# Operands of a 256-token float32 chain moved to chosen places within 256 bytes, with one raw weight buffer fewer and new sequences of matmul passes

## The chip, the cores and the metric

The kernel runs on one core of a Trainium2 chip. The metric is the device time of one execution in microseconds. Three runs of the kernel before gave 797.72, 798.06 and 798.28, median 798.06.

## The reference

Two blocks follow one another on 256 tokens of width 1024, all in float32. Cut to what matters:

```
# first block
q,k,va, qr,kr,vr, gr, ga,gb = split(rms(x) @ w_in)
y  = sigmoid(ga)*(diff_attention(q,k,va) @ wd) + sigmoid(gb)*(silu(gr)*retention(qr,kr,vr) @ wr)
x += y @ wo
x += relu(rms(x) @ w_ff1)**2 @ w_ff2                # 1024 -> 4096 -> 1024: f1, f2
x += sigmoid(rms(x) @ w_pg) * (p @ wp)
x  = rms(x)
# second block
x += (mlstm(rms(x) @ [mq, mk, mv, mo, gates])) @ mw
u, v = causal_conv3(rms(x) @ [ug, uv])              # 2 x 2816 columns
x += (silu(u) * v) @ dn                             # 2816 -> 1024
out = rms(x)
```

## The kernel before

The weights are cut into slabs, mostly of 1024 rows by 256 columns, and each slab into two halves of 128 partitions by 1024 floats (512 KB), 257 halves and 140 MB in all. The order of the halves (`order`) is fixed by a plan. Every half goes through four hands:

- SP's queue carries it from HBM to a tile `raw` (L155, 5 buffers);
- ACT copies it, rounded, to a tile `hi` of type float32r (L167, 6 buffers);
- DVE subtracts: `lo` = raw - hi, float32r too (L179, 6 buffers);
- PE multiplies. The activations are split into a high and a low tile in the same way (hh and hl, h2h and h2l, and so on), and a product is three passes of 256 columns for each 128 rows: high weights with high activations, high weights with low activations, low weights with high activations. So a whole slab of 1024 x 256 takes 48 matmuls of 256 columns, a half slab 24.

In `pe_b` (L230 to L232) the slab's tiles are the stationary operand (weights) and the activations the moving one; q, k, qr, kr, ga, gb, wd, wr, wo, f1, f2, pg, mq, mk, mw, ug, uv go through it. In `pe_a` (L242 to L244) it is the other way round: activations stationary, the slab moving; va, vr, gr, mv, mo. In the down projection dn (`pe_down`, L1366 to L1368) the slab moves as well, in pieces of 512 and 256 columns, over gh and gl. In the profile an operand pair reads `out<-moving,stationary`. The weights of a matmul are loaded by an instruction of their own (PEld in the profile) while the matmul ahead of it runs.

`slot()` is called after each half slab: it lets ACT run to 6 halves ahead of the last half used up (`high_to`), moves the work that waits behind a slab on by a step, and lets DVE do the same (`split_to`). Each subtraction sets free one raw tile, upon which SP issues the transfer of the half five places on (`dma_to(state["split"] + NRAW)`). `at(name, ...)` hangs other work on a slab: its first function puts matmuls on PE after the slab (with `mid=True` after the first half), its second the work of ACT and DVE behind them. `gates2` makes the tile me for the gates of the mLSTM, `gates3_pe` transposes gi and me (L1082, tile pa_g), `gates3_post` copies pa_g to acol (L1087), `decay_pe` and `decay_post` (L1100, L1109) read it for the decay matrix dm.

The tile framework puts the buffers of a pool behind one another. In the built program raw, hi and lo tiles of 4,096 bytes per partition all begin at 128 modulo 256. The "big" tiles, which hold the activations, are 8,224 bytes long, so that each begins 32 bytes further modulo 256 than the one ahead. The place of the operands, in bytes modulo 256, before and after:

| slabs | role of the activations | activations before (high, low) | slab before | activations after | slab after (hi, lo) |
|---|---|---|---|---|---|
| wo | moving | mh 96, ml 160 | 128 | 0 | 192, 64 |
| f1 | moving | h2h 160, h2l 192 | 128 | 0 | all 16 pairs of 0, 64, 128, 192, one per slab |
| f2, third block of rows | moving | ah 128, al 192 | 128 | 0 | all 16 pairs, one per slab |
| mw | moving | hsh 192, hsl 64 | 128 | 0 | 192, 64 |
| ug, uv 2 to 10 | moving | h7h 0, h7l 192 | 128 | 0 | the 16 pairs, two of them twice |
| q, k, qr, kr, ga, gb, pg and the rest of `pe_b` | moving | various multiples of 32 | 128 | 0 | 192, 64 |
| va, vr, gr | stationary | hh 192, hl 160 | 128 | 0 | spread over the pairs |
| mo, mv 1 to 3 | stationary | h4h 32, h4l 224 | 128 | 0 | spread over the pairs |
| dn, second eight blocks of rows | stationary | gh 64, gl 192 | 128 | 0 | spread over the pairs |

Of the kernel before, what the change touches and what calls it, by code (L numbers as in the profile page):

```python
# [10 lines left out]
F32 = mybir.dt.float32  # L11
F32R = mybir.dt.float32r
# [4 lines left out]
P = 128  # L17
T = 256
# [2 lines left out]
LAM_INIT = 0.8 - 0.6 * math.exp(-0.3 * 0)  # L21
LNEXP = "natural_log_exp_and_others"
NBUF = 6
NRAW = 5
NWARM = 9
NRAWUP = 2
JOINT = (("q0", "k0"), ("wo0", "wo1"), ("f1_0", "f1_1"), ("pg0", "pg1"), ("mq0", "mk0"), ("mw0", "mw1"), ("ug0", "uv0"))
NUP = 2816 // 256
NPAR = 65 + 176 + 2

GAINS = [
    ("g_mix", 8), ("g_mlp", 8), ("g_ple", 8), ("g_final", 8), ("l0_norm_mix_2", 8), ("l0_norm_ffn_2", 8),
# [62 lines left out]
def _rows(slab):  # L95

    name, w, k0, nk, cl = slab
    return ((0, 1), (2, 3, 4), (5, 6, 7)) if name == "mv0" else (tuple(range(nk // 2)), tuple(range(nk // 2, nk)))


def _width(slab):
    return 264 if slab[0] == "mv0" else 2048 // slab[3]


@with_exitstack
def block_kernel(ctx: ExitStack, tc: tile.TileContext, I, out):
# [7 lines left out]
    psum = ctx.enter_context(tc.tile_pool(name="psum", bufs=4, space=bass.MemoryType.PSUM))  # L114

    def bigt(name, dt=F32, cols=2048):
        return big.tile([P, 2056], dt, tag="big", name=name)[:, 0:cols]

    def c8(t):
        return t.rearrange("p (c t) -> p c t", t=T)  # L120
# [1 line left out]
    def mmbank(name):  # L122
        return psum.tile([P, 512], F32, tag="mm", name=name)
# [21 lines left out]
    def geometry(i):  # L145
        return len(_rows(slabs[i])[0]), _width(slabs[i])

    def dma_to(n):
        while state["dma"] < min(n, len(order)):
            i, s = order[state["dma"]]  # L150
            name = slabs[i][0]
            kk, cw = len(_rows(slabs[i])[s]), _width(slabs[i])
            raw = wpool.tile([P, 1024], F32, tag="raw", name=f"raw_{name}_{s}", bufs=NRAW)
            v = raw[:, 0:kk * cw].rearrange("p (k n) -> p k n", k=kk)
            nc.sync.dma_start(out=raw[:, 0:kk * cw], in_=I["w"][state["dma"], :, 0:kk * cw])  # L155
            raw_t[i, s] = v
            state["dma"] += 1

    def high_to(n):

        while state["high"] < min(n, len(order)):
            i, s = order[state["high"]]
            kk, cw = len(_rows(slabs[i])[s]), _width(slabs[i])
            dma_to(state["high"] + 1)
            hi = wpool.tile([P, 1024], F32R, tag="hi", name=f"hi_{slabs[i][0]}_{s}", bufs=NBUF)
            hi_t[i, s] = hi[:, 0:kk * cw].rearrange("p (k n) -> p k n", k=kk)
            S.activation(hi_t[i, s], raw_t[i, s], ACTF.Copy)  # L167
            state["high"] += 1

    def split_to(n):  # L170

        while state["split"] < min(n, len(order)):
            i, s = order[state["split"]]
            kk, cw = len(_rows(slabs[i])[s]), _width(slabs[i])
            high_to(state["split"] + 1)
            raw = raw_t.pop((i, s))
            lo = wpool.tile([P, 1024], F32R, tag="lo", name=f"lo_{slabs[i][0]}_{s}", bufs=NBUF)
            lo_t[i, s] = lo[:, 0:kk * cw].rearrange("p (k n) -> p k n", k=kk)
            V.tensor_tensor(out=lo_t[i, s], in0=raw, in1=hi_t[i, s].bitcast(F32), op=ALU.subtract)  # L179
# [40 lines left out]
    def pe_b(ps, i, xh, xl, ks, m, start, stop):  # L220

        kk, cw = geometry(i)
        mc = min(P, cw)
        o = ps[0:mc, m * T:(m + 1) * T]
        for k in ks:
            hv, lv = hi_t[i, k // kk], lo_t[i, k // kk]
            a, x = k % kk, k
            sl = slice(m * P, m * P + mc)
            st, sp = start and k == ks[0], stop and k == ks[-1]
            TE.matmul(o, lhsT=hv[:, a, sl], rhs=xh[:, x, :], start=st, stop=False, skip_group_check=True)  # L230
            TE.matmul(o, lhsT=hv[:, a, sl], rhs=xl[:, x, :], start=False, stop=False, skip_group_check=True)  # L231
            TE.matmul(o, lhsT=lv[:, a, sl], rhs=xh[:, x, :], start=False, stop=sp, skip_group_check=True)  # L232

    def pe_a(ps, i, xh, xl, ks, t, start, stop):

        o = ps[:, t * T:(t + 1) * T]
        ts = slice(t * P, (t + 1) * P)
        for k in ks:
            hv, lv = hi_t[i, k // 4], lo_t[i, k // 4]
            a = k % 4  # L240
            st, sp = start and k == ks[0], stop and k == ks[-1]
            TE.matmul(o, lhsT=xh[:, k, ts], rhs=hv[:, a, :], start=st, stop=False, skip_group_check=True)  # L242
            TE.matmul(o, lhsT=xl[:, k, ts], rhs=hv[:, a, :], start=False, stop=False, skip_group_check=True)
            TE.matmul(o, lhsT=xh[:, k, ts], rhs=lv[:, a, :], start=False, stop=sp, skip_group_check=True)  # L244
# [3 lines left out]
    def at(name, pe=None, post=None, off=0, mid=False):  # L248
        i = index[name] + off
        if mid:  # L250
            hooks_mid.setdefault(i, []).append((pe, post))
            return
        if pe:
            hooks_pe.setdefault(i, []).append(pe)
        if post:
            hooks_post.setdefault(i, []).append(post)
# [23 lines left out]
                        later(i, g)  # L280
                slot()

    def step_b(name, xh, xl, post):
        i = index[name]
        ps = mmbank(f"ps_{name}")

        def piece(s):
            for m in range(2):
                pe_b(ps, i, xh, xl, range(4 * s, 4 * s + 4), m, s == 0 and m == 0, s == 1 and m == 1)

        halves(i, piece)
        after(i, lambda: post(ps))
# [73 lines left out]
    with tc.manual_schedule():  # L366
# [1 line left out]

        x = bigt("x0")
        xT = c8(x)  # L370
        par = const.tile([P, NPAR], F32, name="par")
        nc.scalar.dma_start(out=par[:, 0:8], in_=I["par"][:, 0:8])
        first = [wpool.tile([P, 1024], F32, tag="raw", name=f"raw_{n}", bufs=NRAW) for n in range(4)]
        for c in range(4):
# [83 lines left out]

        sq_new("n1")
        for n in range(4):  # L460
            for tag, dt, d in (("hi", F32R, hi_t), ("lo", F32R, lo_t)):
                t = wpool.tile([P, 1024], dt, tag=tag, name=f"{tag}_{n}", bufs=NBUF)
                d[order[n]] = t.rearrange("p (k n) -> p k n", k=4)
        def first_split(n, ks):
            rv, hv, lv = first[n].rearrange("p (k n) -> p k n", k=4)[:, ks, :], hi_t[order[n]][:, ks, :], lo_t[order[n]][:, ks, :]
            S.activation(hv, rv, ACTF.Copy)
# [111 lines left out]
        va = bigt("va").rearrange("p (t n) -> p t n", t=2)  # L578
# [146 lines left out]
        i, ps0 = index["q0"], [mmbank(f"ps_{n}") for n in ("q0", "k0")]  # L725
# [44 lines left out]
        gr, ga = bigt("gr").rearrange("p (t n) -> p t n", t=2), c8(bigt("ga"))  # L770
# [119 lines left out]
        ah, al = {}, {}  # L890
# [27 lines left out]
        for j in range(4):  # L918
            ps = mmbank(f"ps_f2_{j}")
            for kg in range(4):  # L920
                i = index[f"f2_{j}_{kg}"]

                def piece(s):
                    for m in range(2):
                        pe_b(ps, i, ah[kg], al[kg], range(4 * s, 4 * s + 4), m, kg == 0 and s == 0 and m == 0,
                             kg == 3 and s == 1 and m == 1)

                halves(i, piece)
                after(i, *([lambda j=j, ps=ps: post_res("n3", j, h3h, h3l, "g_ple", r2)(ps)] if kg == 3 else []))
# [5 lines left out]
        i = index["wp"]  # L935
        need(i, 0)
        need(i, 1)
        for j in range(4):
            ps = mmbank(f"ps_wp{j}")
            for m in range(2):  # L940
                o = ps[:, m * T:(m + 1) * T]
                sl = slice((2 * j + m) * P, (2 * j + m + 1) * P)
                for k in range(2):
                    hv, lv = hi_t[i, k], lo_t[i, k]
# [335 lines left out]
        ug, uv = {}, {}  # L1280
# [22 lines left out]
        def post_ug(j):  # L1303
            def f(ps):
                yield from conv(ps, 2 * j, 2 * j, f"g{j}")
                y = ug[j] = pr(ring[:, (2 * j) % 4, :])
                S.activation(y, y, ACTF.Silu)
                if j == NUP - 1:
                    S.preload_act_table_set(LNEXP)
            return f  # L1310

        def post_uv(j):
            def f(ps):
                yield from conv(ps, 22 + 2 * j, 2 * j + 1, f"v{j}")
# [213 lines left out]
```

## Time and profile before

| | |
|---|---|
| median of three runs | 798.06 us |
| the profiled execution | 797.67 us |
| its span | 795.9 us |
| matmuls, and PE's busy time | 6,394, 785.8 us |
| weight loads, busy time | 6,394, 771.2 us |
| DVE, ACT busy | 569.5 us, 464.6 us |
| carried by SP's queue and the others | 141.75 MB, mean 178 GB/s |

The span is what the profile's views cover; the other 1.8 us of the execution lie around it. A matmul's duration in the timeline covers its way through the array and overlaps the next one's, so the cost of a matmul in a long row is the distance from start to start.

### The profile page before, as it was taken

Reading aid. Unit: us, or ns where it says so; the run is one execution under the profiler, and the core shown is the slowest. Engines: PE = TensorE matmul, PEld = TensorE weight load, DVE = VectorE, ACT = ScalarE, POOL = GpSimd, SP = SyncE. Lnnn points to the kernel's source line nnn. Section 1 sums busy time; section 2 is a strip of 40 time slices with the busy share of each in tenths; the row PEclk is TensorE's granted clock in tenths of the full one; section 3 lists DMA queues with packets and bytes.
Section 4 is the critical chain, followed back from the end, with each engine's and each line's share of the span. In section 5 each row is a group of like instructions: output and inputs, shape, how many; then the busy total and the mean of one; then the engine's idle time right before and its main releaser. Section 6 shows DMA issues by size and latency. Waiting matters only on the chain.

```text
span 795.9 us, 15702 instructions
## 1 busy us (share of the span) xinstructions
PE 785.8 (99%) x6394; PEld 771.2 (97%) x6394; DVE 569.5 (72%) x895; ACT 464.6 (58%) x788; POOL 2.2 (0%) x8
## 2 busy tenths in 40 slices
PE   8999999999999999999999999999999999999996
PEld 8999999999999999999999999999999999999885
DVE  6877889566666577666555557897978988987443
ACT  7655656765744456555444456765865766756432
POOL 0000000000000000000000000000000000000000
PEclk9999999999999999999999999999999999999998
DMA  8875453455666556666665545354365457765621
GB/s 305 269 242 161 152 160 123 150 162 163 186 199 189 167 184 192 192 185 188 202 183 184 187 145 179 129 202 157 120 223 160 144 177 234 220 206 163 208 80 53
DMA packets 40472, 141.75 MB, mean 178 GB/s; under 512 B 4640, under 2 KB 5024, under 8 KB 40400
## 3 DMA queue, kind: packets, MB, share of 16 engines
q1 hardware_dynamic: 40032, 140.02, 55.7%
q8 instruction: 50, 0.82, 0.4%
q0 software_dynamic: 224, 0.72, 0.2%
q14 instruction: 22, 0.18, 0.1%
q10 hardware_dynamic: 144, 0.00, 0.0%
HBM read 139.68 MB, written 1.05 MB: 177 GB/s over the span
## 4 chain that ended last, share of the span: by engine, by line
PE 94%; DVE 3%; ACT 1%; DMA 1%; issue 1%; SPq 0%; DVEq 0%
PE ps_f L231 8%; PE ps_f L230 8%; PE ps_f L232 8%; PE ps_uv L230 3%; PE ps_ug L230 3%; PE ps_uv L231 3%; PE ps_ug L231 3%; PE acc L1368 3%; PE acc L1366 3%; PE acc L1367 3%; PE ps_ug L232 3%; PE ps_uv L232 3%; PE ps_vr L242 1%; PE ps_wo L231 1%; PE ps_va L242 1%; PE ps_mo L242 1%
## 5 line engine op out<-in xcount | busy, mean ns | idle before, releaser
L179 DVE TENSOR_TENSOR lo_f<-raw_f,hi_f 128x1024 fp32r<-128x1024 f32 x64 | 77.7, 1223 | 52.8 <-ACT hi_f L167 52.8
L167 ACT ACTIVATE hi_f<-raw_f 128x1024 fp32r<-128x1024 f32 x64 | 67.6, 1060 | 79.6 <-PE ps_f L231 70.3
L231 PE MATMUL ps_f<-al,hi_f 128*128 128x256 f32 x256 | 72.1, 282 | 0.0
L230 PE MATMUL ps_f<-ah,hi_f 128*128 128x256 f32 x256 | 72.0, 281 | 0.0
L232 PE MATMUL ps_f<-ah,lo_f 128*128 128x256 f32 x256 | 72.0, 281 | 0.0
L230 PE MATMUL ps_f<-h2h,hi_f 128*128 128x256 f32 x256 | 71.9, 281 | 0.0
L231 PE MATMUL ps_f<-h2l,hi_f 128*128 128x256 f32 x256 | 71.9, 281 | 0.0
L232 PE MATMUL ps_f<-h2h,lo_f 128*128 128x256 f32 x256 | 71.8, 281 | 0.0
L230 PEld LDWEIGHTS ps_f<-ah,hi_f 128*128 128x128 f32 x256 | 48.3, 189 | 0.0
L230 PEld LDWEIGHTS ps_f<-h2h,hi_f 128*128 128x128 f32 x256 | 48.3, 189 | 0.0
L232 PEld LDWEIGHTS ps_f<-ah,lo_f 128*128 128x128 f32 x256 | 48.3, 189 | 0.0
L231 PEld LDWEIGHTS ps_f<-al,hi_f 128*128 128x128 f32 x256 | 48.2, 188 | 0.0
L231 PEld LDWEIGHTS ps_f<-h2l,hi_f 128*128 128x128 f32 x256 | 48.1, 188 | 0.0
L232 PEld LDWEIGHTS ps_f<-h2h,lo_f 128*128 128x128 f32 x256 | 48.1, 188 | 0.0
L179 DVE TENSOR_TENSOR lo_dn<-raw_dn,hi_dn 128x1024 fp32r<-128x1024 f32 x22 | 26.9, 1223 | 22.8 <-ACT hi_dn L167 22.8
L167 ACT ACTIVATE hi_dn<-raw_dn 128x1024 fp32r<-128x1024 f32 x22 | 23.3, 1060 | 30.7 <-PE acc L1367 24.5
L230 PE MATMUL ps_ug<-h7h,hi_ug 128*128 128x256 f32 x144 | 40.8, 283 | 0.0
L230 PE MATMUL ps_uv<-h7h,hi_uv 128*128 128x256 f32 x144 | 40.5, 282 | 0.0
L231 PE MATMUL ps_uv<-h7l,hi_uv 128*128 128x256 f32 x144 | 40.3, 280 | 0.0
L231 PE MATMUL ps_ug<-h7l,hi_ug 128*128 128x256 f32 x144 | 40.3, 280 | 0.0
L232 PE MATMUL ps_ug<-h7h,lo_ug 128*128 128x256 f32 x144 | 40.0, 278 | 0.0
L232 PE MATMUL ps_uv<-h7h,lo_uv 128*128 128x256 f32 x144 | 40.0, 278 | 0.0
(492 smaller groups left out, 2932.4 us busy)
## 6 DMA issues: line engine op xcount, KB each, us to landing
raw_f<-in_w_dram SPq DMA_DIRECT2D x64, 512.0 KB, 3.6
raw_ug<-in_w_dram SPq DMA_DIRECT2D x22, 512.0 KB, 4.1
raw_uv<-in_w_dram SPq DMA_DIRECT2D x22, 512.0 KB, 4.3
raw_dn<-in_w_dram SPq DMA_DIRECT2D x22, 512.0 KB, 3.6
raw_va<-in_w_dram SPq DMA_DIRECT2D x8, 512.0 KB, 4.8
raw_vr<-in_w_dram SPq DMA_DIRECT2D x8, 512.0 KB, 3.5
raw_gr<-in_w_dram SPq DMA_DIRECT2D x8, 512.0 KB, 3.5
raw_ga<-in_w_dram SPq DMA_DIRECT2D x8, 512.0 KB, 3.6
```

The source lines that it names most:

```text
L167: S.activation(hi_t[i, s], raw_t[i, s], ACTF.Copy)
L179: V.tensor_tensor(out=lo_t[i, s], in0=raw, in1=hi_t[i, s].bitcast(F32), op=ALU.subtract)
L230: TE.matmul(o, lhsT=hv[:, a, sl], rhs=xh[:, x, :], start=st, stop=False, skip_group_check=True)
L231: TE.matmul(o, lhsT=hv[:, a, sl], rhs=xl[:, x, :], start=False, stop=False, skip_group_check=True)
L232: TE.matmul(o, lhsT=lv[:, a, sl], rhs=xh[:, x, :], start=False, stop=sp, skip_group_check=True)
L242: TE.matmul(o, lhsT=xh[:, k, ts], rhs=hv[:, a, :], start=st, stop=False, skip_group_check=True)
L1366: TE.matmul(o, lhsT=gh[b][:, r, ts], rhs=hv[:, 0, ns], start=k == 0, stop=False)
L1367: TE.matmul(o, lhsT=gl[b][:, r, ts], rhs=hv[:, 0, ns], start=False, stop=False)
L1368: TE.matmul(o, lhsT=gh[b][:, r, ts], rhs=lv[:, 0, ns], start=False, stop=k == NK - 1)
```

## The change

1. All buffers get known places. The big tiles grow from 2,056 to 2,112 columns, and the tile par by 32, so that every big, raw, hi and lo buffer begins at 0 modulo 256.
2. The slots for hi and lo grow from 1,024 to 1,088 columns, and a slab's hi and lo tiles begin 0, 64, 128 or 192 bytes into their slots, by a function of the slab's name (`_place`, in units of 64 bytes): hi at 192 and lo at 64 where nothing else is said, and through all sixteen pairs in f1, f2, ug and uv from 2 on, the five kinds of `pe_a`, and dn.
3. The raw buffers go from five to four.
4. f2, and ug and uv from 2 on, run their passes in two other sequences (`pe_b2`). With f1, which keeps its triples, there are three.
5. The transposes of the gates go from the end of mv1 to the middle of mv2, 24 matmuls later.

The number of matmuls, weight loads, copies, subtractions and transfers stays.

PE at the start of f2, on its first 128 rows, before (ps_f2_0 is the bank of the first 256 output columns, ah0 and al0 the high and low activations, hi_f2_0_0_0 and lo_f2_0_0_0 the first half slab):

```order
L230 MATMUL ps_f2_0_4760<-ah0_3822,hi_f2_0_0_0_4603 128x256
L231 MATMUL ps_f2_0_4760<-al0_3823,hi_f2_0_0_0_4603 128x256
L232 MATMUL ps_f2_0_4760<-ah0_3822,lo_f2_0_0_0_4607 128x256
L230 MATMUL ps_f2_0_4760<-ah0_3822,hi_f2_0_0_0_4603 128x256
L231 MATMUL ps_f2_0_4760<-al0_3823,hi_f2_0_0_0_4603 128x256
L232 MATMUL ps_f2_0_4760<-ah0_3822,lo_f2_0_0_0_4607 128x256
```

and after (x2 is two matmuls in a row, one for each 128 of the 256 columns):

```order
L268 MATMUL ps_f2_0_4758<-ah0_3820,hi_f2_0_0_0_4601 128x256 x2
L268 MATMUL ps_f2_0_4758<-ah0_3820,lo_f2_0_0_0_4605 128x256 x2
L268 MATMUL ps_f2_0_4758<-al0_3821,hi_f2_0_0_0_4601 128x256 x2
L268 MATMUL ps_f2_0_4758<-ah0_3820,hi_f2_0_0_0_4601 128x256 x2
L268 MATMUL ps_f2_0_4758<-ah0_3820,lo_f2_0_0_0_4605 128x256 x2
```

The moving tile changes after four matmuls and again after two, where it changed twice in three; high and low weights take turns in pairs.

PE at the start of ug2 (bank ps_ug2, activations h7h and h7l), before:

```order
L230 MATMUL ps_ug2_7839<-h7h_7529,hi_ug2_0_7676 128x256
L231 MATMUL ps_ug2_7839<-h7l_7530,hi_ug2_0_7676 128x256
L232 MATMUL ps_ug2_7839<-h7h_7529,lo_ug2_0_7683 128x256
L230 MATMUL ps_ug2_7839<-h7h_7529,hi_ug2_0_7676 128x256
L231 MATMUL ps_ug2_7839<-h7l_7530,hi_ug2_0_7676 128x256
```

and after:

```order
L268 MATMUL ps_ug2_7837<-h7h_7527,hi_ug2_0_7674 128x256 x4
L268 MATMUL ps_ug2_7837<-h7l_7528,hi_ug2_0_7674 128x256 x4
L268 MATMUL ps_ug2_7837<-h7h_7527,lo_ug2_0_7681 128x256 x4
L268 MATMUL ps_ug2_7837<-h7h_7527,hi_ug2_0_7674 128x256 x4
L268 MATMUL ps_ug2_7837<-h7l_7528,hi_ug2_0_7674 128x256 x4
L268 MATMUL ps_ug2_7837<-h7h_7527,lo_ug2_0_7681 128x256 x4
```

Each pass now runs over four blocks of rows ahead of the next pass.

PE at the gates' transposes, before, with the end of mv1 ahead of them and the start of mv2 behind:

```order
L243 MATMUL ps_mv1_6534<-hi_mv1_1_6412,h4l_5833 128x256
L244 MATMUL ps_mv1_6534<-lo_mv1_1_6425,h4h_5832 128x256
L1082 MATMUL pa_g_6602<-ident_109,gi_6492 128x4
L1082 MATMUL pa_g_6602<-ident_109,me_6567 128x4
L242 MATMUL ps_mv2_6613<-hi_mv2_0_6453,h4h_5832 128x256
```

and after, with mv2's first half ahead and its second half behind:

```order
L280 MATMUL ps_mv2_6606<-hi_mv2_0_6451,h4l_5831 128x256
L281 MATMUL ps_mv2_6606<-lo_mv2_0_6455,h4h_5830 128x256
L1122 MATMUL pa_g_6635<-ident_109,gi_6490 128x4
L1122 MATMUL pa_g_6635<-ident_109,me_6565 128x4
L279 MATMUL ps_mv2_6606<-hi_mv2_1_6488,h4h_5830 128x256
```

They stand 24 matmuls later in PE's row; SP, ACT and DVE keep their rows but for a few neighbours that change places (the constants cD and maskT go ahead of one slab's transfer, the copies mvh and mvl one or two rows up).

The core of the diff:

```
-NRAW = 5
+NRAW = 4
...
+PAD = 32
...
+def _place(name):
+
+    n, j = name[0:2], int(name[-1]) if name[-1].isdigit() else 0
+    if name.startswith("f1_"):
+        j = int(name[3:])
+        return j % 4, j // 4
+    if name.startswith("f2_"):
+        j = 4 * int(name[3]) + int(name[5])
+        return j % 4, j // 4
+    if n in ("va", "vr", "gr", "mv", "mo"):
+        j = (4 * ("va", "vr", "gr", "mo", "mv").index(n) + j) % 16
+        return j % 4, j // 4
+    if n in ("ug", "uv"):
+        j = int(name[2:])
+        if j > 1:
+            j = 2 * (j - 2) + (n == "uv")
+            return j % 4, j // 4 % 4
+    if n == "dn":
+        j = int(name[2:])
+        return j % 4, (j + j // 4) % 4
+    return 3, 1
...
-        return big.tile([P, 2056], dt, tag="big", name=name)[:, 0:cols]
+        return big.tile([P, 2112], dt, tag="big", name=name)[:, 0:cols]
...
+    def slot_of(tag, i, s):
+
+        name = slabs[i][0]
+        kk, cw = len(_rows(slabs[i])[s]), _width(slabs[i])
+        pitch = -(-cw // 64) * 64
+        sh = 16 * _place(name)[tag == "lo"]
+        t = wpool.tile([P, 1088], F32R, tag=tag, name=f"{tag}_{name}_{s}", bufs=NBUF)
+        return t[:, sh:sh + kk * pitch].rearrange("p (k n) -> p k n", k=kk)[:, :, 0:cw]
...
-            hi = wpool.tile([P, 1024], F32R, tag="hi", name=f"hi_{slabs[i][0]}_{s}", bufs=NBUF)
-            hi_t[i, s] = hi[:, 0:kk * cw].rearrange("p (k n) -> p k n", k=kk)
+            hi_t[i, s] = slot_of("hi", i, s)
...
-            lo = wpool.tile([P, 1024], F32R, tag="lo", name=f"lo_{slabs[i][0]}_{s}", bufs=NBUF)
-            lo_t[i, s] = lo[:, 0:kk * cw].rearrange("p (k n) -> p k n", k=kk)
+            lo_t[i, s] = slot_of("lo", i, s)
...
+    def pe_b2(ps, i, xh, xl, ks, start, stop, steps):
+
+        kk, cw = geometry(i)
+        for n, (k, m, q) in enumerate(steps):
+            wv = (lo_t if q == 2 else hi_t)[i, k // kk]
+            TE.matmul(ps[:, m * T:(m + 1) * T], lhsT=wv[:, k % kk, m * P:(m + 1) * P], rhs=(xl if q == 1 else xh)[:, k, :],
+                      start=start and n == 0, stop=stop and n == len(steps) - 1, skip_group_check=True)
...
+            if passes:
+                ks = range(4 * s, 4 * s + 4)
+                pe_b2(ps, i, xh, xl, ks, s == 0, s == 1, [(k, m, q) for m in range(2) for q in range(3) for k in ks])
+                return
...
-        par = const.tile([P, NPAR], F32, name="par")
+        par = const.tile([P, NPAR + PAD], F32, name="par")[:, 0:NPAR]
...
-                    for m in range(2):
-                        pe_b(ps, i, ah[kg], al[kg], range(4 * s, 4 * s + 4), m, kg == 0 and s == 0 and m == 0,
-                             kg == 3 and s == 1 and m == 1)
+                    ks = range(4 * s, 4 * s + 4)
+                    pe_b2(ps, i, ah[kg], al[kg], ks, kg == 0 and s == 0, kg == 3 and s == 1,
+                          [(k, m, q) for k in ks for q in (0, 2, 1) for m in range(2)])
...
-        at("mv1", gates3_pe, gates3_post)
+        at("mv2", gates3_pe, gates3_post, mid=True)
...
-            step_b(f"ug{j}", hv, lv, post_ug(j))
-            step_b(f"uv{j}", hv, lv, post_uv(j))
+            step_b(f"ug{j}", hv, lv, post_ug(j), j >= NRAWUP)
+            step_b(f"uv{j}", hv, lv, post_uv(j), j >= NRAWUP)
```

More of the change, by code (lines that the diff above doesn't have):

```diff
@@ L162, in high_to @@
             i, s = order[state["high"]]
-            kk, cw = len(_rows(slabs[i])[s]), _width(slabs[i])
             dma_to(state["high"] + 1)
-            hi = wpool.tile([P, 1024], F32R, tag="hi", name=f"hi_{slabs[i][0]}_{s}", bufs=NBUF)
-            hi_t[i, s] = hi[:, 0:kk * cw].rearrange("p (k n) -> p k n", k=kk)
+            hi_t[i, s] = slot_of("hi", i, s)
             S.activation(hi_t[i, s], raw_t[i, s], ACTF.Copy)
@@ L173, in split_to @@
             i, s = order[state["split"]]
-            kk, cw = len(_rows(slabs[i])[s]), _width(slabs[i])
             high_to(state["split"] + 1)
             raw = raw_t.pop((i, s))
-            lo = wpool.tile([P, 1024], F32R, tag="lo", name=f"lo_{slabs[i][0]}_{s}", bufs=NBUF)
-            lo_t[i, s] = lo[:, 0:kk * cw].rearrange("p (k n) -> p k n", k=kk)
+            lo_t[i, s] = slot_of("lo", i, s)
             V.tensor_tensor(out=lo_t[i, s], in0=raw, in1=hi_t[i, s].bitcast(F32), op=ALU.subtract)
@@ L281, in halves, with step_b @@
                 slot()
-    def step_b(name, xh, xl, post):
+    def step_b(name, xh, xl, post, passes=False):
         i = index[name]
@@ L460, in block_kernel @@
         for n in range(4):
-            for tag, dt, d in (("hi", F32R, hi_t), ("lo", F32R, lo_t)):
-                t = wpool.tile([P, 1024], dt, tag=tag, name=f"{tag}_{n}", bufs=NBUF)
-                d[order[n]] = t.rearrange("p (k n) -> p k n", k=4)
+            for tag, d in (("hi", hi_t), ("lo", lo_t)):
+                d[order[n]] = slot_of(tag, *order[n])
         def first_split(n, ks):
```

## The prediction

> **What bounds the kernel now.** I read the page from its top: busy time, the row of the clock, the chain that ended last.
>
> ```profile
> PE 785.8 (99%) x6394; PEld 771.2 (97%) x6394; DVE 569.5 (72%) x895; ACT 464.6 (58%) x788; POOL 2.2 (0%) x8
> ...
> PEclk9999999999999999999999999999999999999998
> ...
> PE 94%; DVE 3%; ACT 1%; DMA 1%; issue 1%; SPq 0%; DVEq 0%
> ```
>
> PE is busy for 785.8 of 795.9 us at a full clock, and 94% of the chain lies on it. The change leaves the count of matmuls as it is, so the time moves only if one matmul comes to cost another time, if a stall of PE goes, or if a new one comes. So I asked the timeline what a 256-column matmul costs from start to start, as a mean over a long unbroken row. Each pair below is the first and the last start (us) of such a row; the second column is one matmul's own duration, which overlaps the next.
>
> ```profile
> 273.59 0.28 PE L230 MATMUL ps_wo<-mh,hi_wo 128*128 128x256 f32 x1
> ...
> 279.35 0.28 PE L230 MATMUL ps_wo<-mh,hi_wo 128*128 128x256 f32 x1
> ...
> 330.76 0.28 PE L230 MATMUL ps_f<-h2h,hi_f 128*128 128x256 f32 x1
> ...
> 353.38 0.28 PE L230 MATMUL ps_f<-h2h,hi_f 128*128 128x256 f32 x1
> ...
> 387.34 0.28 PE L230 MATMUL ps_f<-ah,hi_f 128*128 128x256 f32 x1
> ...
> 393.07 0.28 PE L230 MATMUL ps_f<-ah,hi_f 128*128 128x256 f32 x1
> ...
> 542.88 0.28 PE L242 MATMUL ps_mv<-hi_mv,h4h 128*128 128x256 f32 x1
> ...
> 545.03 0.28 PE L242 MATMUL ps_mv<-hi_mv,h4h 128*128 128x256 f32 x1
> ...
> 590.27 0.28 PE L230 MATMUL ps_mw<-hsh,hi_mw 128*128 128x256 f32 x1
> ...
> 595.92 0.28 PE L230 MATMUL ps_mw<-hsh,hi_mw 128*128 128x256 f32 x1
> ...
> 659.92 0.28 PE L231 MATMUL ps_ug<-h7l,hi_ug 128*128 128x256 f32 x1
> ...
> 665.41 0.28 PE L230 MATMUL ps_uv<-h7h,hi_uv 128*128 128x256 f32 x1
> ...
> 768.92 0.28 PE L1366 MATMUL acc<-hi_dn,gh 128*128 128x256 f32 x1
> ...
> 769.60 0.39 PE L1366 MATMUL acc<-hi_dn,gh 128*128 128x512 f32 x1
> ```
>
> Matmuls between the two starts, and the step: wo 48, 120.0 ns; f1 (moving h2h) 192, 117.8; f2's third block of 1024 rows (moving ah) 48, 119.4; mv 18, 119.4; mw 48, 117.7; ug 47, 116.8; down projection 6, 113.3. Shape, type, clock and passes are the same, and each step repeats through its whole row. What differs is where the operands lie, by the table above: wo moves tiles at 96 and 160 over weights at 128; f2's third block 128 and 192 over 128; mw 192 and 64 over 128; ug 0 and 192 over 128. The down projection has the slab as the moving operand, at 128, and gh and gl as weights at 64 and 192. So the place goes with up to 6.7 ns of 120, and the change touches just that. With about 5,600 steps in the kernel, 1 ns of a step is worth some 5 us.
>
> **The slabs at the default places.** 48 slabs (q, k, qr, kr, ga, gb, wd, wr, wo, pg, mq, mk, mw, ug and uv 0 and 1) get moving tiles at 0, high weights at 192, low weights at 64: 48 x 48 = 2,304 matmuls. Counted from the moving operand's place, the weights loaded next lie 64 below, 64 above, 64 below; in the down projection's row gh and gl lie 64 below and above a slab at 128, in the same turn. There too the moving place stays put through the triple. That is the nearest row, so I take 113.3. The four wo slabs gain 192 x 6.7 = 1.3 us. The other 2,112 matmuls I put at f1's 117.8, since mw and ug beside it stand at 117.7 and 116.8: 2,112 x 4.5 = 9.5. From this 10.8 I take back two places where PE is not what sets the pace:
>
> ```profile
> 0.00:20.00 20.00, 17.86 (x123) 17.06 (x124) 13.41 (x26) 14.15 (x25) 1.62 (x7) 1.00 0.86 304
> ...
> 285.00:375.00 90.00, 90.00 (x765) 89.95 (x764) 60.70 (x71) 50.70 (x67) 0.00 (x0) 1.00 0.63 191
> 375.00:466.00 91.00, 91.00 (x770) 91.00 (x770) 49.18 (x51) 39.42 (x44) 0.00 (x0) 1.00 0.60 189
> ...
> 495.00:526.00 31.00, 30.76 (x250) 29.87 (x249) 26.87 (x45) 22.09 (x43) 0.00 (x0) 1.00 0.44 152
> 526.00:578.00 52.00, 50.95 (x416) 49.98 (x416) 44.45 (x107) 36.88 (x87) 0.00 (x0) 1.00 0.47 156
> ...
> 625.00:729.00 104.00, 104.00 (x886) 103.77 (x885) 93.34 (x143) 69.62 (x101) 0.53 (x1) 1.00 0.65 198
> ```
>
> (Stretch, its length, then busy time of PE, weight loads, DVE, ACT and POOL, clock, DMA share, GB/s.) In the first 20 us PE idles 2.1 with the DMA engines 86% full, so q0 and k0 (96 x 4.5 = 0.4) gain nothing. At 495 to 526 (mq, mk) DVE is busy 26.87 of 31 and PE already idles 0.24, so 192 x 4.5 = 0.9 is left out. That leaves 9.5 us. The upper bound is 10.8; the lower is mw's 117.7, whose places differ by 64 as well but with the moving side changing: then only wo gains, 192 x 2.3 = 0.4.
>
> **The slabs whose places are spread.** f1 and f2 (768 matmuls each), ug and uv 2 to 10 (864), and va, vr, gr, mo, mv 1 to 3 (912) run through all sixteen pairs of places 0, 64, 128, 192, with the moving tile (in the last group the weights) at 0. Of a weight at 0 or 128 over a tile at 0 the trace shows no row by itself. The rows in which every place is a multiple of 64 are the down projection's, ug's, mw's and f2's third block's: 113.3, 116.8, 117.7, 119.4, mean 116.8. A survey of all pairs should come near such a mean, so I take it. f1 from 117.8: 768 x 1.0 = 0.8. f2: its window holds 770 matmuls in 91.00 us, 118.2: 768 x 1.4 = 1.1. ug and uv stand at 116.8 already: 0. The last group from mv's 119.4: 912 x 2.6 = 2.4. Sum 4.3. Bounds: all at 113.3 gives 3.5 + 3.8 + 3.0 + 5.6 = 15.9; all at the worst row, 120.0, gives -1.7 - 1.4 - 2.8 - 0.5 = -6.4. The down projection, with gh and gl now at 0 and the slab spread, I leave at 0; by the same two rows it is worth 2% of its 67 us either way at most, about 1.
>
> **The sequences of passes.** The new orders for f2 and for ug and uv change neither the number of matmuls nor of weight loads, and each step still has its own load. Results are added in other turns into the same bank. With the same moving tile kept for four matmuls in a row, the step's moving side alternates less; the down projection's row, where the slab stays for two, is the nearest and it is the fast one. I put 0 and count their part in the bounds of the spread slabs.
>
> **The gates' transposes, half a slab later.**
>
> ```profile
> 532.59 0.22 PE L1082 MATMUL pa_g<-ident,gi 4*128 4x4 f32 x1
> 533.78 0.22 PE L1082 MATMUL pa_g<-ident,me 4*128 4x4 f32 x1 [0.97 <-ACT me L1072]
> ...
> 536.68 0.15 DVE L1087 COPY acol<-pa_g 128x16 f32<-128x16 f32 x1
> ...
> 539.97 0.38 PE L1100 MATMUL mm<-mp,pick 4*128 4x256 f32 x1
> ...
> 540.74 1.13 DVE L1109 SCALAR_TENSOR_TENSOR dm<-mm,acol,maskT 128x256 f32<-128x256 f32 x3 [0.86 <-PE mm L1101]
> ```
>
> PE stood 0.97 us for me. After 24 more matmuls, 24 x 0.119 = 2.9 us, it comes there at 535.4, past me's end at 533.7: 1.0 us gained. The copy acol goes from 536.68 to about 539.5, still ahead of its reader at 540.74, which waits for the decay matmuls anyway. If the copy slips a full half slab more, dm is late by 2 us, beside matmuls of mv and mo; bounds 0 and 1.0.
>
> **One raw buffer fewer.**
>
> ```profile
> SPq L155 <- DVE lo_f L179: 155.5, 64, 5.4
> ...
> ACT hi_va L167 <- DMA raw_va<-in_w_dram: 1.8, 2, 1.6
> ...
> ACT hi_mv L167 <- DMA raw_mv<-in_w_dram: 0.7, 1, 0.7
> ...
> raw_uv<-in_w_dram SPq DMA_DIRECT2D x22, 512.0 KB, 4.3
> ...
> L179 DVE TENSOR_TENSOR lo_f<-raw_f,hi_f 128x1024 fp32r<-128x1024 f32 x64 | 77.7, 1223 | 52.8 <-ACT hi_f L167 52.8
> L167 ACT ACTIVATE hi_f<-raw_f 128x1024 fp32r<-128x1024 f32 x64 | 67.6, 1060 | 79.6 <-PE ps_f L231 70.3
> ```
>
> SP's queue waits for DVE to free a raw buffer at each of f's 64 transfers, so with four each transfer starts one half slab later against its use, 24 x 0.118 = 2.8 us. Behind the waiting issue stand the next slabs' transfers and small constants (cD, maskT), which now start ahead of one slab each. One buffer's cycle is landing 4.3 + copy 1.06 + subtraction 1.22 = 6.6 us, and four give 4 x 2.8 = 11.2, or 10.9 at 113.3. ACT waits for a slab three times in all, 2.5 us with five buffers; elsewhere it waits for PE (70.3 us at f), six high buffers ahead. So the two spots that suffer are va and mv. Each can cost one period, 5.6 in all, if PE has no slack there; nothing, if six split slabs cover it. I take -0.5, near to nothing, since three of 257 transfers are late now.
>
> The moves on ACT and DVE (the copies mvh and mvl a row or two earlier) are hidden by the same six buffers; if that cover is gone, each costs one copy, 1.1. The padding alone issues nothing.
>
> **Sum.** 9.5 + 4.3 + 1.0 - 0.5 = 14.3 from the profiled execution's 797.67 (span 795.9 and 1.8 around it, kept): 783.4. The median of the runs is 0.4 above that execution, so 784.
>
> **The rivals.**
> *The places help nothing.* The default slabs cost mw's 117.7 (its places lie 64 apart too, which speaks for this) and the spread ones the mean of ug, mw and f2's third block, 118.0, since all three have the slab as weights. Then 0.4 from wo, -0.2 + 0.2 - 1.0 + 1.3 from the spread, and 0.5 from gates and buffer: 1.2, so 797. Against it: the one row with weights at 64 and 192 is the fastest. The Trainium skill, "TensorE: Matmul & The Clock Gate", Part 2, "Step-by-step: what each phase is for", has separate read ports for weights and moving data, so that loading the next weights takes nothing from the running matmul. By that rule no place matters and only 1.0 - 0.5 = 0.5 is left, 797.6. The trace disagrees: 113.3 against 120.0 ns.
> *Any place on a multiple of 64 is fast, if the moving side stays put.* Then the spread slabs reach 113.3 too: 9.5 + 15.9 + 0.5 = 25.9, so 772. For it: in the one 113.3 row the moving place is constant, in the slower ones mostly not. Against: ug, with every place a multiple of 64, stands at 116.8, and no row shows a weight at 0.
> *Weights at the moving tile's own place collide.* A quarter of the spread matmuls, 3,312 / 4 = 828, get weights at 0 beside tiles at 0. To end slower by 0.2% they must eat 14.3 + 1.6 = 15.9 us, 19 ns each, a step of 136. A step of 140 is 23.2 above the mean taken and gives 784 + 828 x 23.2 us / 1000 = 803. Against it: f2's third block has tile and weights both at 128 and steps at 119.4.
> *The fourth buffer starves PE.* DVE is busy 93.34 of 104 us at ug and uv; if landings go from 4.3 to over 9 us there, the cycle passes 11.2 and 44 transfers each add the excess; 0.4 us each gives 17.6, so 801. Against it: no landing row comes near 9.
>
> **How the numbers follow.** Forecast 0.60, all places fast 0.17, no help 0.14, collision 0.04, starving 0.05. Range: from the fast rival's 772 to 796, which the forecast's own worst spread (797.67 - (9.5 - 6.4 + 1.0 - 0.5) + 0.4 = 794.5) fills; what lies outside is no help and the slower two. 0.2% (1.6 us) is about what a measurement of this kernel tells from no change. Faster by more: forecast and fast rival but for their tails, and a share of no help, 0.80; within: 0.13; slower: 0.07.
>
> **What will show it.** Right: ga, wd, wr, wo and pg step at 113 to 114 ns; f1's and f2's step changes from slab to slab with the places, mean near 117; no wait at pa_g; few waits of ACT for raw. Wrong: ga or wo at 117 or more sinks the main term; slabs with weights at 0 above 130 show the collision; idle time of PE in front of q1, mq or ug, with ACT waiting for raw, the buffer.

## The result and the profile after

The changed kernel takes 790.81 us (790.46 to 791.22), the one before 798.06: ratio 0.991, 95% interval 0.9893 to 0.9927. It is faster by 7.25 us, inside the range of 772 to 796, and by half of the 14.3 that the sum gave. The profiled execution's span is 789.0 us (795.9 before).

From the page of the changed kernel, busy time and the chain that ended last:

```profile
PE 777.8 (99%) x6394; PEld 763.1 (97%) x6394; DVE 569.0 (72%) x895; ACT 464.7 (59%) x788; POOL 2.2 (0%) x8
...
PE 96%; ACT 1%; DVE 1%; DMA 1%; issue 0%; SPq 0%
```

PE's busy time fell by 8.0 us with the same 6,394 matmuls, and PE holds 96% of the chain: the time went out of the matmuls' step. The windows show where. First a stretch of the kernel before that the prediction does not show, then three of the changed kernel (same columns):

```profile
150.00:285.00 135.00, 135.00 (x1141) 134.89 (x1140) 87.51 (x121) 75.38 (x110) 0.00 (x0) 1.00 0.56 172
```

```profile
150.00:285.00 135.00, 135.00 (x1180) 134.89 (x1179) 90.01 (x125) 78.19 (x115) 0.00 (x0) 1.00 0.57 180
285.00:375.00 90.00, 90.00 (x764) 89.95 (x763) 60.82 (x71) 50.78 (x67) 0.00 (x0) 1.00 0.61 191
375.00:466.00 91.00, 91.00 (x776) 91.00 (x775) 49.37 (x51) 39.93 (x46) 0.00 (x0) 1.00 0.61 189
```

At 285 to 375 (f1) 764 matmuls fit where 765 did, at 375 to 466 (f2) 776 where 770 did: next to nothing. At 150 to 285 (the end of gr, then ga to wo) 1,180 started in the same 135 us, where 1,141 did before. Now the timeline, first and last start of unbroken rows, all three with high weights at 192, low weights at 64 and moving tiles at 0:

```profile
268.65 0.28 PE L259 MATMUL ps_wo<-mh,hi_wo 128*128 128x256 f32 x1
...
273.75 0.28 PE L259 MATMUL ps_wo<-mh,hi_wo 128*128 128x256 f32 x1
...
319.66 0.28 PE L259 MATMUL ps_f<-h2h,hi_f 128*128 128x256 f32 x1
...
325.36 0.28 PE L259 MATMUL ps_f<-h2h,hi_f 128*128 128x256 f32 x1
...
478.48 0.28 PE L259 MATMUL ps_pg<-h3h,hi_pg 128*128 128x256 f32 x1
...
484.19 0.28 PE L259 MATMUL ps_pg<-h3h,hi_pg 128*128 128x256 f32 x1
```

wo: 45 matmuls, 113.3 ns. f1's slab 7: 48, 118.8. pg: 48, 119.0. At the same places one family steps at 113.3 and another at 119, and each holds its step over the whole slab. Over the 48 slabs at these places, 31 run at 113.3, 12 at 118.9 (q1, k2, q3, qr0, qr1, kr0, all of pg, ug1, uv1), and 5 change in mid-slab, each where PE waits or does other work in between (mq0, mk0 and mq1, and ug0, uv0). So places do not give one step.

The steps of f1's sixteen slabs in the changed kernel, from the starts in its trace (ns, mean of the slab):

| low \ high | 0 | 64 | 128 | 192 |
|---|---|---|---|---|
| 0 | 119.8 | 117.9 | 118.3 | 117.7 |
| 64 | 117.7 | 117.8 | 117.6 | 118.9 |
| 128 | 119.1 | 118.0 | 118.7 | 115.6 |
| 192 | 117.8 | 114.2 | 119.8 | 117.7 |

The one with high weights at 64 and low at 192 came to 113.3 within its first dozen matmuls; its mirror at 192 and 64 stood at 118.9.

The waits (us in total, times, longest):

```profile
ACT hi_va L198 <- DMA raw_va<-in_w_dram: 2.3, 3, 1.8
...
ACT hi_mv L198 <- DMA raw_mv<-in_w_dram: 1.9, 3, 1.0
...
ACT hi_q L198 <- DMA raw_q<-in_w_dram: 1.4, 1, 1.4
...
PE my L595 <- DVE w_m L584: 1.2, 1, 1.2
```

ACT waits 5.6 us for transfers where it was 2.5. The wait at pa_g is gone, and a new one of 1.2 us stands a little later, where PE multiplies for an mLSTM head (my) and needs its w_m from DVE.

### The profile page after: what moved, and what is told of

Read it like the earlier page. It is cut to its first block, busy times and chain, and to the rows that moved or that the text cites. A ratio compares the mean times of both kernels' runs of the same rounds, so it can differ in the third digit from the quotient of the medians.

```text
span 789.0 us, 15702 instructions
## 1 busy us (share of the span) xinstructions
PE 777.8 (99%) x6394; PEld 763.1 (97%) x6394; DVE 569.0 (72%) x895; ACT 464.7 (59%) x788; POOL 2.2 (0%) x8
## 4 chain that ended last, share of the span: by engine, by line
PE 96%; ACT 1%; DVE 1%; DMA 1%; issue 0%; SPq 0%
PE ps_f L268 11%; PE ps_ug L268 6%; PE ps_uv L268 6%; PE ps_f L259 4%; PE ps_f L260 4%; PE ps_f L261 4%; PE acc L1407 3%; PE acc L1408 3%; PE acc L1406 3%; PE ps_vr L279 1%; PE ps_va L279 1%; PE ps_gr L281 1%; PE ps_va L281 1%; PE ps_mo L281 1%; PE ps_va L280 1%; PE ps_mo L279 1%
## 5 line engine op out<-in xcount | busy, mean ns | idle before, releaser
L268 PE MATMUL ps_f<-ah,hi_f 128*128 128x256 f32 x256 | 51.1, 281 | 0.0
L268 PE MATMUL ps_f<-ah,lo_f 128*128 128x256 f32 x256 | 50.9, 280 | 0.0
L268 PE MATMUL ps_f<-al,hi_f 128*128 128x256 f32 x256 | 50.9, 280 | 0.0
L268 PEld LDWEIGHTS ps_f<-ah,lo_f 128*128 128x128 f32 x256 | 39.3, 189 | 0.0
L1407 PE MATMUL acc<-hi_dn,gl 128*128 128x512 f32 (+1 forms) x110 | 38.3, 348 | 0.0
L1408 PE MATMUL acc<-lo_dn,gh 128*128 128x512 f32 (+1 forms) x110 | 38.3, 348 | 0.0
L1406 PE MATMUL acc<-hi_dn,gh 128*128 128x512 f32 (+1 forms) x110 | 38.2, 348 | 0.0
L208 DVE TENSOR_TENSOR lo_ug<-raw_ug,hi_ug 128x1024 fp32r<-128x1024 f32 x22 | 26.5, 1221 | 6.0 <-ACT hi_ug L198 6.0
L198 ACT ACTIVATE hi_ug<-raw_ug 128x1024 fp32r<-128x1024 f32 x22 | 22.8, 1052 | 8.5 <-PE ps_uv L268 4.8
L208 DVE TENSOR_TENSOR lo_uv<-raw_uv,hi_uv 128x1024 fp32r<-128x1024 f32 x22 | 26.7, 1219 | 1.2 <-ACT hi_uv L198 1.2
```

Of the source, the lines that this page charges most:

```text
L268: TE.matmul(ps[:, m * T:(m + 1) * T], lhsT=wv[:, k % kk, m * P:(m + 1) * P], rhs=(xl if q == 1 else xh)[:, k, :], start=start and n == 0, ...
L1406: TE.matmul(o, lhsT=gh[b][:, r, ts], rhs=hv[:, 0, ns], start=k == 0, stop=False)
L1407: TE.matmul(o, lhsT=gl[b][:, r, ts], rhs=hv[:, 0, ns], start=False, stop=False)
L1408: TE.matmul(o, lhsT=gh[b][:, r, ts], rhs=lv[:, 0, ns], start=False, stop=k == NK - 1)
```

## The experiments

Theory A: the pair of places sets the step, and something beside them held some families back. Theory B: at some places a row of matmuls has two steps that hold themselves, and what stands ahead of the row chooses between them.

**All at 192 and 64.**

```
 def _place(name):
-    ... (by slab)
+    return 3, 1
```

> The changed kernel with one edit: every slab has its high weights at 192 and its low weights at 64, so no place is spread any more. Theory A (the pair of places alone sets the step; the default slabs that stood at 118.9 in the changed kernel had something else in their way): f1, f2, ug and uv come to 113.3 wherever ga to wo did, 3.5 + 3.4 + 3.5 us less than the 790.8 of the changed kernel, about 780, while pg stays at 118.9. Theory B (at 192 and 64 a row of matmuls has two steps that hold themselves, 113.3 and 118.9, and what stands ahead of the row chooses): no middle values; f1 follows wo without a break and stays at 113.3, but other families come out at the one or the other, and some that were fast may be slow: anywhere from 778 to 796, with families at 113.3 or 118.9 only.

783.83 us, ratio 0.9824 (0.981 to 0.9837). Apart from mv0, whose slab is wider, no slab had a steady step other than 113.3 or 118 to 119. f1 followed wo at 113.3 and lost it in the middle of its slab 2, at two matmuls of a norm's statistics (pv_n). Timeline:

```profile
289.98 0.28 PE L240 MATMUL ps_f<-h2h,hi_f 128*128 128x256 f32 x1
...
292.36 0.28 PE L240 MATMUL ps_f<-h2h,hi_f 128*128 128x256 f32 x1
...
292.70 0.59 PE L899 MATMUL pv_n<-sqs_n,ones 128*128 128x256 f32 x2
...
301.34 0.28 PE L240 MATMUL ps_f<-h2h,hi_f 128*128 128x256 f32 x1
...
369.82 0.28 PE L240 MATMUL ps_f<-h2h,hi_f 128*128 128x256 f32 x1
```

Ahead of pv_n 21 matmuls at 113.3; from 301.34 to 369.82, 576 at 118.9, with no break in between. f2, at 113.4 on the mean, came out of that slow row within its first dozen matmuls, with its other sequence of passes. This speaks for B.

**All at 64 and 192.**

```
-    return 3, 1
+    return 1, 3
```

> The changed kernel with every slab's high weights at 64 and low weights at 192. All four slabs that had this pair in the changed kernel (f1_13, one of f2, uv8 and f2's last but three) came to 113.3 out of rows at 118. Theory B with a choice by the row's start: if this pair leaves the slow step by itself, all families in pe_b come to 113.3, pg, q, k and ug1 too: 790.8 - 10.4 (f1, f2, ug, uv) - 1.1 (pg) - 1.2 (q, qr, kr, k) - 0.5 (ug1, uv1) = about 777.5. Theory A (places alone): the same as with 192 and 64 by symmetry, about 780, with pg still at 118.9.

777.57 us, ratio 0.9747 (0.9733 to 0.976), as theory B with a pair that leaves the slow step by itself gave it. The same break in f1, in this kernel's timeline:

```profile
291.37 0.59 PE L899 MATMUL pv_n<-sqs_n,ones 128*128 128x256 f32 x2
...
299.99 0.28 PE L240 MATMUL ps_f<-h2h,hi_f 128*128 128x256 f32 x1
...
359.49 0.28 PE L240 MATMUL ps_f<-h2h,hi_f 128*128 128x256 f32 x1
```

525 matmuls behind the break at 113.3. Every family of pe_b comes back to it within some 12 matmuls of a break, pg and ug1 too (part of mq0 is broken too often to get that far). Only three slabs of the changed kernel had this pair, f1_13, f2_3_1 and uv8, and not four as the expectation counts; f2_1_3, which came to 113.3 there too, stood at 192 and 64. The mirror image in places is no mirror image in time. High weights are loaded twice in three, and here these lie above the moving tile; that this is the reason is likely, but no run shows it by itself.

**Triples again.**

```
-            step_b(f"ug{j}", hv, lv, post_ug(j), j >= NRAWUP)
+            step_b(f"ug{j}", hv, lv, post_ug(j))
```
(uv and f2 likewise)

> The changed kernel with its places, but f2 and ug and uv back in triples (high by high, high by low, low by high for each 128 rows). If the sequences of passes do nothing: 790.8 within 1 us, each slab of f2 and ug at the step that f1's slab with the same pair shows. If they help: f2's and uv's slabs at 192,64 and 64,192 (113.3 now) go to the 119 that f1_7 shows at 192,64, and the time rises by some 1 to 2 us.

791.33 us (0.9905 to 0.9932 of before), against 790.81. In the profiled executions, 791.8 against 790.84, f2 lost 0.16 and ug and uv 0.21 by the sums of the starts: the sequences are worth some 0.4 us. Another 0.7 came from q, k, mq and mk, whose code is the same: q0 and k0, at 113 in the changed kernel, stood at 119 here. So even the same instructions ahead of a row do not settle its step, where the row starts on a wait. Of the slabs at 192 and 64, f2_1_3 went to 119 as f1_7 had, but uv5 stayed at 113.3 in triples too, and so did the two at 64 and 192 (f2_3_1, uv8): the second expectation held for one slab of four.

**The two small parts alone.**

```
-NRAW = 5
+NRAW = 4
-        at("mv1", gates3_pe, gates3_post)
+        at("mv2", gates3_pe, gates3_post, mid=True)
```

> The kernel before with two parts of the change alone: four raw buffers, and the gates' transposes half a slab later. Places and passes as before. The forecast's terms: -1.0 from the gates, +0.5 from the buffer, so 797.6. From the changed kernel's trace: the 1.0 us of waiting at pa_g is gone but 1.2 us appear where PE waits for w_m, and ACT waits for transfers 5.6 us where it was 2.5; if both hold here, 798.3 to 799.

798.02 us, ratio 1.0002 (0.9993 to 1.0011): nothing. Its waits:

```profile
ACT hi_mv L167 <- DMA raw_mv<-in_w_dram: 2.2, 3, 1.2
...
ACT hi_mo L167 <- DMA raw_mo<-in_w_dram: 1.6, 1, 1.6
...
PE my L555 <- DVE w_m L544: 0.9, 1, 0.9
```

**Each of the two by itself.** The same diff, one line at a time.

> The kernel before with the gates' transposes half a slab later and nothing else (five raw buffers). Theory D (DVE's own row sets when w_m is ready, so that PE gains nothing by passing pa_g earlier): no wait at pa_g, about 1.0 us of waiting at my for w_m, 798.0 as before. Rival E (the wait at my comes from the missing raw buffer, which held hi_mo back by 1.6 us): no wait at my, and 797.0.

797.45 us, ratio 0.9994 (0.9985 to 1.0003). Its waits:

```profile
PE my L555 <- DVE w_m L544: 0.2, 1, 0.2
```

> The kernel before with four raw buffers and nothing else. Theory D: the 5 to 7 us that ACT then waits for transfers lie under its six buffers' lead, so 798.0 within 0.5, with the wait at pa_g as before. Rival E: some of it reaches PE, 798.5 to 799.5.

799.78 us, ratio 1.0018 (1.0009 to 1.0027); its runs fall into two groups, five at 798.2 to 798.8 and six at 799.8 to 800.2, and the profiled one is of the lower. There PE's wait at pa_g grew from 1.0:

```profile
PE pa_g L1082 <- ACT me L1072: 1.4, 1, 1.4
```

So rival E holds for the most part. By the start of PE's last matmul the gates' move alone gains 0.8 (1.0 at pa_g, 0.2 given back at my), the buffer alone costs 0.5, and with both the missing buffer makes DVE late. DVE's timeline shows the second w_m, the one that my waits for, in the kernel with the gates alone

```profile
546.05 0.55 DVE L544 TENSOR_TENSOR w_m<-ms,dm 128x384 f32<-128x384 f32 x1
```

and with both:

```profile
546.77 0.55 DVE L544 TENSOR_TENSOR w_m<-ms,dm 128x384 f32<-128x384 f32 x1
```

0.7 us later, which is the difference of the two waits at my. The delay does not begin at hi_mo, as rival E had it, but at hi_mv: with both, ACT waits 2.0 us for two transfers of mv at 525 to 528, where it waited 0.5 with the gates alone. The gates' tile gl, next in ACT's row, starts at 529.12 instead of 527.40, and me behind it at 534.14 instead of 533.43.

The two groups of the buffer's runs differ in PE's clock. Over the execution it was granted 0.998 of full speed in each of the five shorter runs and 0.994 to 0.996 in each of the six longer ones; 0.2% of 796 us is 1.6 us, the distance between the groups (the two runs at 0.994 are no longer than those at 0.996, so not all of the lost clock costs time). At the same clock, then, the buffer alone costs 0.4 us (798.35, the median of the five, against 797.95) and not 1.8. No longer run of this kernel was profiled, but one of a later kernel was (the gates back behind mv1, below).

**A break put in.** The kernel at 192 and 64, with

```
+        def stir():
+            ps = aux("stir")
+            for t in range(4):
+                TE.transpose(ps[:, 4 * t:4 * t + 4], ident[0:4, 0:P], ident[0:4, 0:4])
+        for n in (4, 7, 10, 13):
+            at(f"f1_{n}", stir)
```

> The kernel with 192 and 64 everywhere, and four tiny transposes (into a tile that nobody reads) after f1_4, f1_7, f1_10 and f1_13. There f1 ran at 113.3 up to the middle of f1_2 and at 118.9 in all that follows, without a break. Theory B: each break chooses anew, so some of the four pieces behind a break come to 113.3 (if all four do, 12 slabs x 48 x 5.5 ns = 3.0 us less than 783.8, plus 4 breaks at 0.3); a break after which a row changes its step at unchanged places would show that the start decides. Theory A and any theory of what runs beside f1 (DMA, ACT, DVE): 118.9 to the end of f1, and 1.2 us more, 785.

Timeline around the first two breaks:

```profile
301.45 0.28 PE L240 MATMUL ps_f<-h2h,hi_f 128*128 128x256 f32 x1
...
306.81 0.28 PE L240 MATMUL ps_f<-h2h,hi_f 128*128 128x256 f32 x1
...
307.25 0.41 PE L930 MATMUL stir<-ident 4*128 4x4 f32 x4
...
308.04 0.28 PE L240 MATMUL ps_f<-h2h,hi_f 128*128 128x256 f32 x1
...
323.68 0.28 PE L240 MATMUL ps_f<-h2h,hi_f 128*128 128x256 f32 x1
...
324.11 0.40 PE L930 MATMUL stir<-ident 4*128 4x4 f32 x4
...
324.91 0.28 PE L240 MATMUL ps_f<-h2h,hi_f 128*128 128x256 f32 x1
...
330.26 0.28 PE L240 MATMUL ps_f<-h2h,hi_f 128*128 128x256 f32 x1
```

45 matmuls at 119, break, 138 at 113.3, break, 45 at 119; the third break led to 113.3 again and the fourth to 119. Places and code are the same on both sides of a break, and what runs beside f1 is work of the same kind: the break turns the step. This settles B against A. The time was 784.77 (0.9826 to 0.9853 of before), 0.9 more than without breaks: in f1 the six slabs at the fast step gained 1.6, but the four breaks cost 0.54 each, 2.2 together. In the profiled execution ug and uv, whose code is untouched, also came out 2.1 us slower (786.59; the other runs took 784.25 to 784.98, about that much less).

**Only differences, or places too?** Moving tiles at 64 by the first edit, with weights at 128 and 0; and in another kernel weights 32 bytes to both sides:

```
-        return big.tile([P, 2112], dt, tag="big", name=name)[:, 0:cols]
+        return big.tile([P, 2112], dt, tag="big", name=name)[:, 16:16 + cols]
-    return 1, 3
+    return 2, 0
```

> All activation tiles begin 64 bytes further (at 64), high weights at 128 and low weights at 0: every difference as in the kernel with 64 and 192 over 0, every place itself another. If only differences count: 777.6 within 1.5 us and 113.3 throughout pe_b. If the places themselves count (say 64 and 192 as weights, or 0 as the moving place): f1, f2, ug and uv away from 113.3, 785 to 795.

777.65 us, ratio 0.9745 (0.9732 to 0.9759), the same as unshifted. f1:

```profile
318.90 0.28 PE L240 MATMUL ps_f<-h2h,hi_f 128*128 128x256 f32 x1
...
341.00 0.28 PE L240 MATMUL ps_f<-h2h,hi_f 128*128 128x256 f32 x1
```

195 at 113.3. For this pair the difference counts, not the place.

```
-        sh = 16 * _place(name)[tag == "lo"]
+        sh = 8 * _place(name)[tag == "lo"]
-    return 1, 3
+    return 1, 7
```

> High weights 32 bytes above the moving tile and low weights 32 below (32 and 224 over 0) for every slab, else as the kernel with 64 and 192. If any constant moving place with weights off to both sides does: 777.6 within 2 us. If 64 is the unit that counts: no row at 113.3, f1, f2, ug and uv at 117 to 120, 788 to 798.

799.03 us, ratio 1.0014 (1.0004 to 1.0023). f1:

```profile
330.87 0.28 PE L240 MATMUL ps_f<-h2h,hi_f 128*128 128x256 f32 x1
...
353.57 0.28 PE L240 MATMUL ps_f<-h2h,hi_f 128*128 128x256 f32 x1
```

192 at 118.2, and no row at 113.3 anywhere: 32 bytes to both sides do not do it.

**pe_a and the down projection.**

```
+    if name[0:2] in ("va", "vr", "gr", "mv", "mo"):
+        return 3, 3
+    if name[0:2] == "dn":
+        return 0, 0
     return 1, 3
...
+        at = 16 if name.startswith("gh") else 48 if name.startswith("gl") else 0
-        return big.tile([P, 2112], dt, tag="big", name=name)[:, 0:cols]
+        return big.tile([P, 2112], dt, tag="big", name=name)[:, at:at + cols]
```

> High weights at 64 and low at 192 for every slab of pe_b, as in the last kernel but one; for va, vr, gr, mv and mo the slab's high and low tiles both at 192 over activations at 0, as mo3 had them in the changed kernel, where it stood at 114.0; in dn both at 0, with gh at 64 and gl at 192. If a constant moving place with the weights 64 bytes off is what lets a row come to 113.3, the five groups of pe_a go from 117.7 to 113.3 (912 x 4.4 = 4.0 us) and dn gains 1 to 1.5 us: 777.6 - 5.3 = about 772.3. Rival: mo3 was fast by its start alone and 192 under 0 leaves both steps possible: pe_a's groups then come out at 113 or 118 to 119, and the time at 773 to 777.

774.49 us, ratio 0.9706 (0.9693 to 0.9719): the rival's case. The timeline of two neighbouring slabs of gr:

```profile
145.01 0.28 PE L265 MATMUL ps_gr<-hi_gr,hh 128*128 128x256 f32 x1
...
148.90 0.28 PE L265 MATMUL ps_gr<-hi_gr,hh 128*128 128x256 f32 x1
...
152.93 0.28 PE L265 MATMUL ps_gr<-hi_gr,hh 128*128 128x256 f32 x1
...
156.67 0.28 PE L265 MATMUL ps_gr<-hi_gr,hh 128*128 128x256 f32 x1
```

33 at 117.9 and 33 at 113.3: two steps here as well. dn's 256-column pieces came from 116.9 (all at 64 and 192) to 113.3, and dn gained 0.6 us.

**The gates back, and the fifth buffer back, on this fastest version.**

```
-        at("mv2", gates3_pe, gates3_post, mid=True)
+        at("mv1", gates3_pe, gates3_post)
```

> The fastest kernel so far (64 and 192 for pe_b, 192 and 192 for pe_a, gh and gl 64 to both sides) with the gates' transposes back behind mv1. Theory D: the 1.3 us at my go and about as much comes back at pa_g, 774.5 within 0.5. Were the later place worth what was forecast for it: 775.5.

774.96 us, ratio 0.9714 (0.9701 to 0.9728), against 774.49 with the later place: not told apart. In the profiled execution the waits at pa_g are 1.4 + 0.4, and at my 0.3 where it had been 1.3. But that execution is the longest of the four (776.19 at a granted clock of 0.996; the others took 774.71 to 775.01 at 0.997 to 0.998), and its windows show why:

```profile
510.00:518.40 8.40, 6.62 (x56) 6.31 (x56) 7.39 (x14) 4.80 (x9) 0.00 (x0) 1.00 0.71 236
518.40:521.90 3.50, 3.50 (x19) 3.50 (x18) 3.50 (x5) 1.98 (x4) 0.00 (x0) 0.51 0.42 110
521.90:530.00 8.10, 8.10 (x66) 7.74 (x65) 5.99 (x14) 4.54 (x6) 0.00 (x0) 1.00 0.61 211
```

Less than 1 us after the waits at pa_g the clock is halved for 3.4 us, 19 matmuls start where 30 would have, and PE loses 1.3 us. This made PE late at my too, so the 0.3 there is not the work of the gates' place alone. The buffer alone waits at pa_g in the same way, so its longer runs are likely to hold such a stretch; that they do, and that the wait is what brings it on, no run shows.

```
-NRAW = 4
+NRAW = 5
...
-        t = wpool.tile([P, 1088], F32R, tag=tag, name=f"{tag}_{name}_{s}", bufs=NBUF)
+        t = wpool.tile([P, 1088 if tag == "hi" else 1024], F32R, tag=tag, name=f"{tag}_{name}_{s}", bufs=NBUF)
```
(a 192-byte tile ahead of the low slots, which puts them all at 192, dn's places shifted with them, and two scratch tiles single)

> The places of the fastest kernel so far (774.5) with five raw buffers again: the room comes from low slots without padding (all at 192, so dn's high tiles go there too, over gh at 0 and gl at 128, the same differences) and from two scratch tiles single instead of double. From the two single parts on the kernel before (buffer alone +1.8, gates alone -0.5, both +0.1): the fifth buffer is worth 0.6 to 1.8 us, so 772.7 to 773.9, with the wait at my down from 1.3 to a few tenths. If the fifth buffer matters only under slower steps, or the single scratch tiles hold up ACT, 774.5 or more.

774.01 us, ratio 0.97 (0.9687 to 0.9713): the fastest, 23.9 us below the kernel before and 16.8 below the change. The fifth buffer gave 0.5 at most, less than the 0.6 to 1.8 expected, whose upper end rested on the two groups of runs above, and no more than the difference that the gates' place left undecided. The wait at my stayed at 1.1; that PE is early there because its steps are shorter is likely, but was not tested.

## Why the prediction was right or wrong

- **What bounds.** Right: PE's step moved the time. Its busy time fell by 8.0 us, of which waits took back 0.5.
- **The 24 slabs ga, gb, wd, wr, wo, mw** at the default places: 960 x 4.5 + 192 x 6.7 = 5.6 us of the sum; their starts show 5.5. The down projection's fast row gave the right step for them, and that was luck. It is one of eight such rows in the kernel before, one for each of the second eight blocks of rows, at the same places. Five run at 113.3, but the first two at 118.3 and 116.7 and the last at 114.2. The first of the eight:

```profile
752.39 0.28 PE L1366 MATMUL acc<-hi_dn,gh 128*128 128x256 f32 x1
...
753.10 0.40 PE L1366 MATMUL acc<-hi_dn,gh 128*128 128x512 f32 x1
```

So the model row itself had more than one step, and the prediction took the fastest. That these 24 slabs came out fast and pg slow is nothing that it could tell.
- **The other 24 slabs at the default places** (q, k, qr, kr, pg, mq, mk, ug and uv 0 and 1): 3.9 us of the sum, 1.3 measured. This step failed: it took one pair of places for one step. pg, with nothing in its way, went from 117.8 to 119.0, and the experiment with breaks shows why: these places allow 113.3 and 118.9, and the row's start chooses. A second warning stood in a row that was used as a rival: mw had differences of 64 and stepped at 117.7.
- **The spread slabs**: 4.3 in the sum; 1.0 measured (f1 -0.1, f2 0.55, ug and uv 2 to 10 -0.4, pe_a 1.0). Failed too: the mean of four rows, 116.8, held one row of the fast step among three slow ones, while of sixteen pairs in f1 one reached 113.3 and the mean is 117.9. The rival that any multiple of 64 is fast fails on the same table: at 0, 0 the row stands at 119.8.
- **The sequences of passes** at 0: 0.4 us, right within what can be told.
- **Gates and buffer**: +1.0 and -0.5 in the sum. Alone they change the time by -0.8 and +0.5 in the traces (by the medians -0.5, and +0.4 at the same clock), but together they cancel, since the missing buffer delays DVE's w_m by 0.7 us and PE meets that instead. The prediction looked at acol and dm as next in line and not at w_m two steps on.
- **Rivals.** Collision at place 0 did not come: the row at 0 over 0 costs 119.8, not 136. Starving did not come. That no place matters fails too: the kernels all at 192, 64 and all at 64, 192 differ in nothing but the places, and in time by 6.3 us (783.83 and 777.57). The prediction had drawn this rival from the Trainium skill's two independent read ports ("TensorE: Matmul & The Clock Gate", Part 2, "Step-by-step: what each phase is for"). The time of a step here does not follow what it drew from them; whether the ports are separate no run here shows.

The sum with measured terms: 5.5 + 1.3 + 1.0 + 0.2 (dn) = 8.0, the fall of PE's busy time; less 0.5 (waits and all else) it is 7.5, PE's gain from its first to its last matmul. The time fell inside the range because the 24 slabs brought their 5.5; of the other two large terms a third and a quarter came.

## What to carry to other kernels

Where weights are reloaded for every matmul, treat the distance between the moving operand and the weights loaded behind it, modulo 256 bytes, as a tuning knob, and look at each family's step from start to start, since busy shares stay at 99% either way. Look for places that come back to the fast step by themselves, not for ones that can reach it: here 64 above for two loads of three and 64 below for the third. Where the runs of one kernel fall into groups, look at the granted clock of each before giving a price to the edit. Before two edits that touch the same stretch are summed, ask which third engine both make late.

## What the runs showed of the hardware that was not expected

One sequence of float32r matmuls of 256 columns, at one clock and one set of places, runs at 113.3 or at 118.9 ns a step, holds either for hundreds of matmuls (576 in the longest unbroken row at 118.9), and is turned from one to the other by four tiny transposes. High weights 64 bytes above and low weights 64 below the moving tile returned to 113.3 in every unbroken row that was long enough. The reverse, in triples, kept whichever step it had over the whole of a long row; with f2's sequence of passes it too came to 113.3, in both kernels that had it throughout. What in a row's start chooses the step, and what in the chip holds it, no run here shows.
